# Transposing the gated units of both token halves in one run of eight, in the first four chunks of every feed-forward layer

## The chip, the core and the metric

The kernel runs on one core of a Trainium2 chip. TensorE (PE in the profile) multiplies and transposes and writes PSUM, eight banks of 128 x 512 fp32. PEld is TensorE's loading of the stationary operand, which overlaps PE. VectorE (DVE) and ScalarE (ACT) read PSUM and work on SBUF. SyncE (SP) issues nearly all transfers, and GpSimd (POOL) a few. The metric is the device time of one execution in microseconds; lower is better.

## The reference, cut to what matters

Two stacks run on 256 tokens of width 1024 in fp32. Six token mixers (convolutions, pooling, attention, mLSTM) stand between eight feed-forward layers, and the change touches these eight alone:

```
f = (silu(h @ w_gate) * (h @ w_up)) @ w_down      # h: 256 x 1024, hidden width 2816
```

Before and after each feed-forward layer there is an RMS norm and a residual sum.

## The kernel before, in words

Precision. TensorE works with fp32r operands. Every fp32 operand is split into a high part (a cast on ACT) and a low part (a subtraction on DVE), and every product is three matmuls: high by high, low of the activations by high of the weights, high by low (`mm3`, L282 to L284, in this order). Weights are split on the fly: a raw tile of 1 MB arrives by DMA (L150), ACT casts it in two halves (L229), DVE subtracts in two halves (L190).

Feed-forward. The hidden width is cut into five chunks of 512 and one of 256. The tokens are two halves of 128, h = 0 and h = 1. For a chunk c, gate and up products are made for both halves, ACT and DVE turn them into gated units `s` (128 tokens x 512), and `hidden` transposes each half's `s` in four 128 x 128 blocks into one PSUM bank (L511), splits the bank into high and low (ACT L291, then DVE L292) and gives the bank back. The result is the stationary operand of `down(c, h)`, which is worked off in the middle of the next chunk. Chunk 0 is made by `gate_up`, chunks 1 and 3 by `both`, chunks 2 and 4 (`SUMS`) by `seven`: seven products instead of eight, of operands that DVE adds beforehand. These sums of weight tiles are `pre_add` (DVE L181, in place on a raw tile, when both raw tiles have landed).

What sets the order. There is no planner. Each triple of matmuls is a tick; a tick may issue one step of the weights' splitting, and then runs every task whose delay is over. `hidden` starts such a task, 11 ticks after its half's gated units in chunks 0, 1 and 3, 12 in chunks 2 and 4, 3 in the last chunk. `down` joins the task before it uses its result. Every engine takes its instructions in the order in which they were issued, so a subtraction L292 stands on DVE behind whatever weight step was issued before it, also when that step still waits for a transfer.

Buffers. `ps` are the eight banks, `r2` six tiles for split units (two per half), `f2` ten tiles for units, `r8` nineteen tiles for raw and split weights. All are handed out first come, first served, so a bank that comes back is soon written again: in `seven`, the third product's bank Y (`Y = self.ps.get()`) is one that the chunk before had transposed into.

Of the kernel before, what the change touches and what calls it, by code (L numbers as in the profile page):

```python
# [28 lines left out]
SUMS = (2, 4)  # L29
# [21 lines left out]
class Core:  # L51
# [443 lines left out]
    def ffn(self, plan, half, nxt):  # L495
# [6 lines left out]
        hT, tt = {}, {}  # L502

        def hidden(s, c, h, n, delay):

            def T():
                while not self.ps.free or len(self.r2.free) < 2:
                    yield 1
                b = self.ps.get()
                for j in range(n // 128):  # L510
                    nc.tensor.transpose(out=b[:, j * 128:(j + 1) * 128], in_=s[:, j * 128:(j + 1) * 128], identity=self.ident)  # L511
                self.f2.put(s)
                hT[c, h] = (self.r2.get(), self.r2.get())
                self.split(hT[c, h][0][:, 0:n], hT[c, h][1][:, 0:n], b[:, 0:n])
                self.ps.put(b)
                yield
            tt[c, h] = self.spawn(T(), delay)

        def gate_up(c, h):
            if c < 5:  # L520
                banks = [self.ps.get(), self.ps.get()]
                for i, p in enumerate(G[c]):
                    w = self.need(p)
                    for k in range(4):
                        kk = 4 * (i % 2) + k
                        self.mm3(banks[i // 2], self.lhs(xT, kk, h), (w[0][:, k], w[1][:, k]), kk == 0, kk == 7)
                    if h:
                        self.done(p)
                gb, ub, n = banks[0], banks[1], 512
            else:  # L530
                b = self.ps.get()
                banks = [b]
                for i, p in enumerate(G[c]):
                    w = self.need(p)
                    for k in range(4):
                        kk = 4 * i + k
                        self.mm3(b, self.lhs(xT, kk, h), (w[0][:, k], w[1][:, k]), kk == 0, kk == 7)
                    if h:
                        self.done(p)
                gb, ub, n = b[:, 0:256], b[:, 256:512], 256  # L540
            s = self.f2.get()
            nc.scalar.activation(out=s[:, 0:n], in_=gb, func=ACTF.Silu, scale=rr[h])
            nc.vector.scalar_tensor_tensor(out=s[:, 0:n], in0=ub, scalar=rr[h], in1=s[:, 0:n], op0=ALU.mult, op1=ALU.mult)
            self.ps.put(*banks)
            hidden(s, c, h, n, 11 if c < 5 else 3)

        def both(c):

            s = {}

            def half_chunk(q, use):
                b = [self.ps.get(), self.ps.get()]
                for i in range(2):
                    p = G[c][2 * q + i]
                    w = self.need(p)
                    for h in range(2):
                        for k in range(4):
                            kk = 4 * i + k
                            self.mm3(b[h], self.lhs(xT, kk, h), (w[0][:, k], w[1][:, k]), kk == 0, kk == 7)
                        if i:  # L560
                            self.spawn(use(h, b[h]), 1)
                    self.done(p)

            def gate(h, b):
                s[h] = self.f2.get()
                nc.scalar.activation(out=s[h], in_=b, func=ACTF.Silu, scale=rr[h])
                self.ps.put(b)
                yield

            def up(h, b):  # L570
                nc.vector.scalar_tensor_tensor(out=s[h], in0=b, scalar=rr[h], in1=s[h], op0=ALU.mult, op1=ALU.mult)  # L571
                self.vector(512)
                self.ps.put(b)
                hidden(s[h], c, h, 512, 11)
                yield

            for q, use in enumerate((gate, up)):
                half_chunk(q, use)
                for h in range(2):
                    down(c - 1, h, (q,))  # L580

        def seven(c):


            U = G[c]
            X, Z = self.ps.get(), self.ps.get()
            left = {"a11": lambda k: self.lhs(xT, k, 0), "a12": lambda k: self.lhs(xT, 4 + k, 0), "a22": lambda k: self.lhs(xT, 4 + k, 1)}
            for j, n in enumerate(("s1", "s2", "s4", "s3")):
                left[n] = lambda k, j=j: tuple(t[:, j * 512 + k * 128:j * 512 + k * 128 + 128] for t in self.xs)

            def product(b, n, a, first=False):
                w = self.need(U[n])
                for k in range(4):
                    self.mm3(b, left[a](k), (w[0][:, k], w[1][:, k]), first and k == 0, k == 3, more=not first)
                self.done(U[n])

            f = {}

            def copy(n, b):
                f[n] = self.f2.get()  # L600
                nc.scalar.copy(out=f[n], in_=b)  # L601
                yield

            def gate0():
                nc.vector.tensor_tensor(out=f["1"], in0=Z, in1=f["1"], op=ALU.add)
                self.vector(512)
                self.ps.put(Z)
                nc.scalar.activation(out=f["1"], in_=f["1"], func=ACTF.Silu, scale=rr[0])
                yield

            def up0():
                nc.vector.tensor_tensor(out=f["2"], in0=Y, in1=f["2"], op=ALU.add)
                self.vector(512)
                self.ps.put(Y)
                nc.vector.scalar_tensor_tensor(out=f["2"], in0=f["2"], scalar=self.nr[0], in1=f["1"], op0=ALU.mult, op1=ALU.mult)
                self.vector(512)
                self.f2.put(f["1"])
                hidden(f["2"], c, 0, 512, 12)
                yield

            def up1():
                nc.vector.tensor_tensor(out=f["5"], in0=X, in1=f["5"], op=ALU.add)
                self.vector(512)
                yield

            def gate1():
                g = self.f2.get()
                nc.scalar.activation(out=g, in_=X, func=ACTF.Silu, scale=rr[1])
                self.ps.put(X)
                nc.vector.scalar_tensor_tensor(out=f["5"], in0=f["5"], scalar=self.nr[1], in1=g, op0=ALU.mult, op1=ALU.mult)  # L630
                self.vector(512)
                self.f2.put(g)
                hidden(f["5"], c, 1, 512, 12)
                yield

            product(X, "b11", "a11", True)
            e1 = self.spawn(copy("1", X), 2)
            product(Z, "b21", "a12", True)
            self.join(e1)
            e2 = self.spawn(gate0(), 2)  # L640
            Y = self.ps.get()
            product(Y, "t1", "s1", True)
            e3 = self.spawn(copy("5", Y), 2)
            product(X, "t2", "s2")
            e4 = self.spawn(copy("2", X), 2)
            down(c - 1, 0, (0,))
            self.join(e2, e3)
            product(Y, "b22", "s4")
            self.join(e4)
            e5 = self.spawn(up0(), 2)  # L650
            product(X, "t3", "s3")
            e6 = self.spawn(up1(), 0)
            down(c - 1, 1, (0,))
            down(c - 1, 0, (1,))
            down(c - 1, 1, (1,))
            self.join(e5, e6)
            product(X, "t4", "a22")
            if c == SUMS[-1]:
                self.join(self.spawn(gate1()))
            else:  # L660
                self.spawn(gate1(), 1)
# [22 lines left out]
        def end(h):  # L684
            self.chain(h, acc[h], half, nxt, [lambda: self.ps.put(*acc[h])])

        gate_up(0, 0)
        self.join(self.xt[1])
        rr[1] = self.rr[1]
        gate_up(0, 1)  # L690
        self.ahead = 5
        for c in range(1, 5):
# [11 lines left out]
        down(4, 0)  # L704
        self.limit, self.ahead = 6, 4
        gate_up(5, 0)
        down(4, 1, (0,))
        gate_up(5, 1)
# [1035 lines left out]
```

## Time and profile before

| | us |
|---|---|
| three runs | 2118.84, 2120.30, 2120.38 (median 2120.3) |
| the profiled execution | 2121.1 |
| its span | 2119.1 |
| PE busy | 2094.2 (99%) |
| PEld busy | 1691.5 (80%) |
| DVE busy | 1558.0 (74%) |
| ACT busy | 1213.0 (57%) |
| DMA queue of the weights | 372.04 MB, 50.2% of the 16 engines |

How to read it: the profiled execution took 2121.1 us, of which 2119.1 are the span from the first to the last instruction. A share is a mean over the whole run; whether a particular instruction is late is read in the timeline. A matmul's recorded length (some 400 ns) is longer than the distance to the next one's start (some 233 ns), because matmuls overlap. So the idle time in front of a late matmul is shorter than what its lateness costs.

### The profile page before, as it was taken

The page shows a single profiled execution, that of the slowest core. Times are in us where ns is not written, and L with a number is a line of the kernel's source. Part 1 is how long each engine was busy: PE and PEld are TensorE (multiplying, and loading weights), DVE is VectorE, ACT ScalarE, POOL GpSimd, SP SyncE. Part 2 cuts the span into 40 slices and gives each one's busy share as a digit, 9 for nine tenths or more (in the row PEclk, how much of TensorE's full clock was granted, in tenths as well). Part 3 has the DMA queues.
Part 4 walks back from the last instruction along what each step waited for, and adds up shares of the span by engine and source line. Part 5 has one row for each costly group of instructions (what it writes and reads, how often), then busy time and mean ns, then how long its engine had stood idle before and what let it go on. Part 6 is the DMA issues. An engine that isn't in the chain of part 4 may idle for free. (4 is left out here: it accounts for less than half of the span.)

```text
span 2119.1 us, 25044 instructions
## 1 busy us (share of the span) xinstructions
PE 2094.2 (99%) x9659; PEld 1691.5 (80%) x9659; DVE 1558.0 (74%) x2017; ACT 1213.0 (57%) x1742; POOL 73.7 (3%) x129
## 2 busy tenths in 40 slices
PE   9999999999999999999999999999999999999998
PEld 6877777887888888888888887878888878787887
DVE  5678678876577776678777774787778776479775
ACT  5565456655665555556555456775556545667553
POOL 0000000000000000000000002010000001000000
PEclk9999999999999999999999999999999999999999
DMA  7555554646444564545555464344564545344542
GB/s 279 201 186 196 182 198 151 226 164 222 143 142 173 212 226 162 197 169 199 198 189 177 151 236 163 120 144 174 209 225 162 209 176 184 130 167 161 179 164 95
DMA packets 175623, 383.75 MB, mean 181 GB/s; under 512 B 10428, under 2 KB 29116, under 8 KB 175504
## 3 DMA queue, kind: packets, MB, share of 16 engines
q1 hardware_dynamic: 172592, 372.04, 50.2%
q0 software_dynamic: 2624, 9.58, 1.3%
q8 instruction: 76, 1.25, 0.2%
q10 hardware_dynamic: 288, 0.52, 0.1%
q14 instruction: 43, 0.35, 0.1%
HBM read 380.28 MB, written 1.84 MB: 180 GB/s over the span
## 5 line engine op out<-in xcount | busy, mean ns | idle before, releaser
L282 PE MATMUL ps<-r,r 128*128 128x512 f32 (+1 forms) x2748 | 1100.6, 400 | 2.2 <-ACT f L601 2.2
L283 PE MATMUL ps<-r,r 128*128 128x512 f32 (+1 forms) x2748 | 1082.9, 394 | 3.9 <-DVE r L292 2.6
L284 PE MATMUL ps<-r,r 128*128 128x512 f32 (+1 forms) x2748 | 1080.6, 393 | 2.4 <-DVE r L190 2.4
L190 DVE TENSOR_TENSOR r<-r,r 128x1024 fp32r<-128x1024 f32 x798 | 935.5, 1216 | 167.2 <-ACT r L229 164.4
L229 ACT CAST r<-r 128x1024 fp32r<-128x1024 f32 x798 | 791.8, 1043 | 377.7 <-DVE r L181 163.2
L284 PEld LDWEIGHTS ps<-r,r 128*128 128x128 f32 x2748 | 515.6, 188 | 124.6 <-DVE r L190 7.0
L283 PEld LDWEIGHTS ps<-r,r 128*128 128x128 f32 x2748 | 516.0, 188 | 122.2 <-DVE r L292 11.9
L282 PEld LDWEIGHTS ps<-r,r 128*128 128x128 f32 x2748 | 516.2, 188 | 115.2 <-ACT f L601 2.6
L181 DVE TENSOR_TENSOR r<-r,r 128x1024 f32<-128x1024 f32 x128 | 150.9, 1220 | 57.6 <-DMA r<-in_ffn_w_in_dram 30.3
L291 ACT CAST r<-ps 128x512 fp32r<-128x512 f32 (+1 forms) x108 | 60.0, 555 | 153.2 <-PE ps L511 144.5
L292 DVE TENSOR_TENSOR r<-ps,r 128x512 fp32r<-128x512 f32 (+1 forms) x108 | 69.5, 646 | 89.8 <-ACT r L291 89.8
L571 DVE SCALAR_TENSOR_TENSOR f<-ps,rr,f 128x512 f32<-128x512 f32 x32 | 23.9, 747 | 75.5 <-PE ps L284 75.5
L291 ACT CAST r<-f 128x512 fp32r<-128x512 f32 x84 | 51.4, 619 | 44.2 <-DVE f L376 26.4
L312 POOL TENSOR_TENSOR st<-st,c_mhalf 128x1 f32<-128x1 f32 x28 | 15.9, 569 | 1551.8 <-DVE st L311 1551.4
L316 ACT ACTIVATE c_junk<-x 128x512 bf16<-128x512 f32 x56 | 35.3, 631 | 54.4 <-DVE x L349 53.5
L292 DVE TENSOR_TENSOR r<-f,r 128x512 fp32r<-128x512 f32 x84 | 55.7, 688 | 3.2 <-ACT r L291 0.8
L511 PEld LDWEIGHTS ps<-c_ident,f 128*128 128x128 f32 x352 | 44.3, 140 | 13.2
L511 PE MATMUL ps<-c_ident,f 128*128 128x128 f32 x352 | 54.0, 272 | 0.0
L376 DVE TENSOR_TENSOR f<-ps,c_pre 128x512 f32<-128x512 f32 x52 | 33.5, 685 | 24.3 <-PE ps L302 24.3
L349 DVE SCALAR_TENSOR_TENSOR x<-f,st,x 128x512 f32<-128x512 f32 x56 | 39.6, 749 | 2.5 <-POOL st L312 0.9
L316 ACT ACTIVATE c_junk<-ps 128x512 bf16<-128x512 f32 x52 | 31.0, 597 | 17.0 <-PE ps L284 16.2
L341 DVE TENSOR_TENSOR f<-ps,gn 128x512 f32<-128x512 f32 x52 | 35.5, 683 | 6.7 <-ACT c_junk L316 6.7
(194 smaller groups left out, 940.3 us busy)
## 6 DMA issues: line engine op xcount, KB each, us to landing
r<-in_ffn_w_in_dram SPq DMA_DIRECT2D x80, 1024.0 KB, 5.3
r<-in_ffn_w_down_dram SPq DMA_DIRECT2D x44, 1024.0 KB, 6.2
r<-in_ffn_w_out_dram SPq DMA_DIRECT2D x44, 1024.0 KB, 7.2
r<-in_ffn_w_gate_dram SPq DMA_DIRECT2D x40, 1024.0 KB, 5.3
r<-in_ffn_w_up_dram SPq DMA_DIRECT2D x40, 1024.0 KB, 5.8
r<-in_mix_w_in_dram SPq DMA_DIRECT2D x28, 1024.0 KB, 5.1
r<-in_conv_w_in_dram SPq DMA_DIRECT2D x22, 1024.0 KB, 5.3
r<-in_attn_w_qkv_dram SPq DMA_DIRECT2D x12, 1024.0 KB, 5.3
```

Of the source, the lines that this page charges most:

```text
L181: self.nc.vector.tensor_tensor(out=a[:, sl], in0=a[:, sl], in1=b[:, sl], op=ALU.add)
L190: eng.tensor_tensor(out=lo, in0=raw, in1=hi.bitcast(F32), op=ALU.subtract)
L229: self.nc.scalar.copy(out=hi[:, sl], in_=raw)
L282: mm(out=out, lhsT=x[0], rhs=w[0], start=first, stop=False, skip_group_check=more)
L283: mm(out=out, lhsT=x[1], rhs=w[0], start=False, stop=False, skip_group_check=more)
L284: mm(out=out, lhsT=x[0], rhs=w[1], start=False, stop=last, skip_group_check=more)
L291: self.nc.scalar.copy(out=hi, in_=src)
L292: self.nc.vector.tensor_tensor(out=lo, in0=src, in1=hi.bitcast(F32), op=ALU.subtract)
L316: self.nc.scalar.activation(out=self.junk[:, 0:src.shape[-1]], in_=src, func=ACTF.Square, scale=scale, accum_out=acc)
L341: mul = lambda n: nc.vector.tensor_tensor(out=mg[n], in0=src[n], in1=g[:, n * 512:(n + 1) * 512], op=ALU.mult)
L349: nc.vector.scalar_tensor_tensor(out=xs, in0=mg[n], scalar=r, in1=xs, op0=ALU.mult, op1=ALU.add)
L511: nc.tensor.transpose(out=b[:, j * 128:(j + 1) * 128], in_=s[:, j * 128:(j + 1) * 128], identity=self.ident)
```

## The change

`hidden_pair` takes the place of `hidden` in chunks 0 to 3. It keeps the units of h = 0 until those of h = 1 are ready, then starts one task with the delay that each half had. The task waits until two banks and four `r2` tiles are free, transposes both halves one after the other (through `transpose4`, whose line is L302), and then issues both splits. Chunk 4 and the last chunk keep `hidden`. Whichever half's `down` comes first joins the one task.

```
+        pair = {}
+
+        def hidden_pair(s, c, h, delay):
+
+            pair[h] = s
+            if not h:
+                return
+
+            def T():
+                while len(self.ps.free) < 2 or len(self.r2.free) < 4:
+                    yield 1
+                done = []
+                for i in range(2):
+                    done.append((i, self.transpose4(pair[i])))
+                for i, b in done:
+                    self.f2.put(pair.pop(i))
+                    hT[c, i] = (self.r2.get(), self.r2.get())
+                    self.split(hT[c, i][0], hT[c, i][1], b)
+                    self.ps.put(b)
+                yield
+            tt[c, 0] = tt[c, 1] = self.spawn(T(), delay)
...
-            hidden(s, c, h, n, 11 if c < 5 else 3)
+            if c < 5:
+                hidden_pair(s, c, h, 11)
+            else:
+                hidden(s, c, h, n, 3)
...
-                hidden(s[h], c, h, 512, 11)
+                hidden_pair(s[h], c, h, 11)
...
-                hidden(f["2"], c, 0, 512, 12)
+                if c == SUMS[-1]:
+                    hidden(f["2"], c, 0, 512, 12)
+                else:
+                    hidden_pair(f["2"], c, 0, 12)
...
-                hidden(f["5"], c, 1, 512, 12)
+                if c == SUMS[-1]:
+                    hidden(f["5"], c, 1, 512, 12)
+                else:
+                    hidden_pair(f["5"], c, 1, 12)
```

No instruction is added or removed on any engine; rows move. Below, the second feed-forward layer stands for all eight, in which the places are the same.

DVE, end of chunk 2, before. `r2_5_3161` is the low part of the units of h = 1, `r2_1_3059` (the first row) that of h = 0; `r8` are weights.

```order
L292 TENSOR_TENSOR r2_1_3059<-ps_3_3053,r2_0_3058 128x512
L190 TENSOR_TENSOR r8_16_3050<-r8_3_3009,r8_4_3049 128x1024 x2
L190 TENSOR_TENSOR r8_14_3079<-r8_10_3026,r8_8_3078 128x1024
L630 SCALAR_TENSOR_TENSOR f2_9_2932<-f2_9_2932,rr1_2501,f2_0_3095 128x512
L190 TENSOR_TENSOR r8_14_3079<-r8_10_3026,r8_8_3078 128x1024
L190 TENSOR_TENSOR r8_18_3107<-r8_0_3073,r8_13_3106 128x1024 x2
L190 TENSOR_TENSOR r8_12_3136<-r8_3_3104,r8_5_3135 128x1024 x2
L181 TENSOR_TENSOR r8_3_3104<-r8_3_3104,r8_0_3133 128x1024 x2
L292 TENSOR_TENSOR r2_5_3161<-ps_3_3155,r2_4_3160 128x512
```

The same place after (the lines after the new function have moved by 25 and more; L658 is L630). `r2_1_3157` is now the low part of h = 0.

```order
L190 TENSOR_TENSOR r8_16_3053<-r8_3_3009,r8_11_3052 128x1024 x2
L190 TENSOR_TENSOR r8_14_3070<-r8_10_3029,r8_8_3069 128x1024 x2
L658 SCALAR_TENSOR_TENSOR f2_9_2930<-f2_9_2930,rr1_2501,f2_0_3092 128x512
L190 TENSOR_TENSOR r8_4_3089<-r8_0_3067,r8_13_3088 128x1024 x2
L190 TENSOR_TENSOR r8_12_3127<-r8_3_3086,r8_5_3126 128x1024 x2
L181 TENSOR_TENSOR r8_3_3086<-r8_3_3086,r8_0_3124 128x1024 x2
L292 TENSOR_TENSOR r2_1_3157<-ps_1_3146,r2_0_3156 128x512
L292 TENSOR_TENSOR r2_5_3161<-ps_7_3151,r2_4_3160 128x512
```

The subtraction of h = 0 has moved behind eight halves of weight subtractions and behind the two pre-adds L181.

PE at the same place, after: the run of eight, the first three of the nine matmuls that follow it, and the first three of `down(2, 0)`, which read `r2_0_3156` and `r2_1_3157`.

```order
L302 MATMUL ps_1_3146<-c_ident_71,f2_8_2952 128x128 x4
L302 MATMUL ps_7_3151<-c_ident_71,f2_9_2930 128x128 x4
L282 MATMUL ps_0_3082<-r8_9_3017,r8_1_2374 128x512
L283 MATMUL ps_0_3082<-r8_9_3017,r8_17_2375 128x512
L284 MATMUL ps_0_3082<-r8_7_3018,r8_1_2374 128x512
...
L282 MATMUL ps_2_2701<-r8_15_3034,r2_0_3156 128x512
L283 MATMUL ps_2_2701<-r8_15_3034,r2_1_3157 128x512
L284 MATMUL ps_2_2701<-r8_18_3035,r2_0_3156 128x512
```

Before, the four transposes of h = 0 stood 57 matmuls further ahead, with 70 matmuls between them and the first reader; the four of h = 1 stood where the second half of the run stands now, with 21 matmuls to theirs.

DVE, chunk 1 to chunk 2 of the first feed-forward layer, before: `r2_5_1332` is h = 0, `r2_1_1365` h = 1.

```order
L292 TENSOR_TENSOR r2_5_1332<-ps_5_1326,r2_4_1331 128x512
L190 TENSOR_TENSOR r8_11_1343<-r8_4_1340,r8_16_1342 128x1024
L181 TENSOR_TENSOR r8_6_1245<-r8_6_1245,r8_2_1247 128x1024 x2
L190 TENSOR_TENSOR r8_11_1343<-r8_4_1340,r8_16_1342 128x1024
L292 TENSOR_TENSOR r2_1_1365<-ps_2_1359,r2_0_1364 128x512
```

And after:

```order
L190 TENSOR_TENSOR r8_11_1334<-r8_4_1331,r8_16_1333 128x1024
L181 TENSOR_TENSOR r8_6_1245<-r8_6_1245,r8_2_1247 128x1024 x2
L190 TENSOR_TENSOR r8_11_1334<-r8_4_1331,r8_16_1333 128x1024
L292 TENSOR_TENSOR r2_5_1361<-ps_5_1350,r2_4_1360 128x512
L292 TENSOR_TENSOR r2_1_1365<-ps_2_1355,r2_0_1364 128x512
```

The subtraction that empties the bank of h = 0 has moved behind four weight steps. That bank is now the one that Y gets, 12 matmuls after the run of eight.

## Rows read from the trace of the kernel before

**Rows 1.** The page: busy time, share of the span, instructions.
```profile
PE 2094.2 (99%) x9659; PEld 1691.5 (80%) x9659; DVE 1558.0 (74%) x2017; ACT 1213.0 (57%) x1742; POOL 73.7 (3%) x129
```

**Rows 2.** Waits of PE: who waited for whom, us in total, times, longest.
```profile
PE ps L302 <- DVE x L349: 3.1, 3, 1.9
PE ps L302 <- DVE r L806: 3.0, 1, 3.0
PE ps L283 <- DVE r L292: 2.6, 4, 1.1
...
PE ps L282 <- ACT f L601: 2.2, 1, 2.2
```

**Rows 3.** Timeline of PE, second layer, end of chunk 2: start, length, instruction.
```profile
419.45 0.39 PE L284 MATMUL ps<-r,r 128*128 128x512 f32 x1
419.68 0.60 PE L511 MATMUL ps<-c_ident,f 128*128 128x128 f32 x4
...
420.59 0.39 PE L284 MATMUL ps<-r,r 128*128 128x512 f32 x1
...
422.44 0.39 PE L283 MATMUL ps<-r,r 128*128 128x512 f32 x1
...
425.00 0.39 PE L282 MATMUL ps<-r,r 128*128 128x512 f32 x1
425.46 0.50 PE L283 MATMUL ps<-r,r 128*128 128x512 f32 x1
425.81 0.39 PE L284 MATMUL ps<-r,r 128*128 128x512 f32 x1
```

**Rows 4.** Timeline of PE, a run of eight transposes elsewhere in the kernel.
```profile
113.37 0.39 PE L284 MATMUL ps<-r,r 128*128 128x512 f32 x1
113.60 1.03 PE L302 MATMUL ps<-c_ident,x 128*128 128x128 f32 x8
...
114.94 0.40 PE L284 MATMUL ps<-r,r 128*128 128x512 f32 x1
```

**Rows 5.** Timeline of DVE, second layer, end of chunk 2; idle before, releaser.
```profile
422.45 2.36 DVE L181 TENSOR_TENSOR r<-r,r 128x1024 f32<-128x1024 f32 x2 [2.73 <-DMA r<-in_ffn_w_up_dram]
424.73 0.68 DVE L292 TENSOR_TENSOR r<-ps,r 128x512 fp32r<-128x512 f32 x1
```

**Rows 6.** Timeline of SP's DMA issues, same place.
```profile
416.58 0.37 SPq L150 DMA_DIRECT2D r<-in_ffn_w_up_dram  x1
```

**Rows 7.** Last layer, same place: PE, then DVE.
```profile
2029.70 0.40 PE L283 MATMUL ps<-r,r 128*128 128x512 f32 x1
...
2031.64 0.68 DVE L292 TENSOR_TENSOR r<-ps,r 128x512 fp32r<-128x512 f32 x1
```

**Rows 8.** First layer, chunk 1 to 2: ACT, DVE, PE (Y's first matmul).
```profile
175.91 2.00 ACT L229 CAST r<-r 128x1024 fp32r<-128x1024 f32 x2 [4.15 <-DMA r<-in_ffn_w_down_dram]
...
181.54 0.68 DVE L292 TENSOR_TENSOR r<-ps,r 128x512 fp32r<-128x512 f32 x1
...
176.97 0.40 PE L282 MATMUL ps<-r,r 128*128 128x512 f32 x1
```

**Rows 9.** Second layer, chunk 1 to 2: PE, ACT, DVE, PE (Y's first matmul).
```profile
378.21 0.40 PE L283 MATMUL ps<-r,r 128*128 128x512 f32 x1
...
379.80 2.00 ACT L229 CAST r<-r 128x1024 fp32r<-128x1024 f32 x2
...
385.43 0.68 DVE L292 TENSOR_TENSOR r<-ps,r 128x512 fp32r<-128x512 f32 x1
...
385.09 0.40 PE L282 MATMUL ps<-r,r 128*128 128x512 f32 x1
```

**Rows 10.** Windows after three PE waits: length, engines' busy us, PEclk (granted), DMA.
```profile
33.60:37.00 3.40, 3.26 (x10) 2.79 (x11) 0.10 (x3) 2.11 (x4) 0.00 (x0) 0.50 1.05 387
...
316.90:320.30 3.40, 3.37 (x14) 2.81 (x13) 3.31 (x8) 2.86 (x7) 0.00 (x0) 0.50 0.02 5
...
187.60:191.00 3.40, 3.35 (x14) 2.74 (x15) 3.40 (x4) 3.40 (x5) 0.00 (x0) 1.00 1.05 391
```

## The prediction

> **What bounds the kernel now.** I read the page's busy shares first, then PE's waits, then the timeline around the transposes on PE, DVE and ACT, last the granted clock. TensorE is busy 99% of the span [rows 1], and all its waits together are some 16 us; the four that matter here are in [rows 2]. So a change can win only what TensorE's own instructions cost less, plus a few us of waits, and it can lose wherever an operand comes later than TensorE wants it. Both questions are about single places, not about shares.
>
> **The transposes themselves.** In [rows 3] the reader is to see a run of four between two L284: from 419.45 to 420.59, 1.14 us with three matmul steps in it. The eight steps from 420.59 to 422.44 take 1.85 us, 0.231 each, so the run costs 1.14 - 0.69 = 0.45 us. The run of eight in [rows 4] costs 114.94 - 113.37 - 0.69 = 0.88 us by the same sum. Twice four is 0.90, once eight 0.88: a run has no fixed price that could be saved. 32 runs are merged (four chunks, eight layers), which gives 32 x 0.02 = 0.6 us at most, within the rounding of the rows, and I take 0. The Trainium skill, page "TensorE: Matmul & The Clock Gate", section "Part 4: PE-mode transpose", gives about 275 ns for one transpose in a kernel, most of it access latency. If every run paid that latency once, merging would save 32 x (0.275 - 0.109) = 5.3 us, an estimate from that page; the trace disagrees, since its run of eight costs what two of four do.
>
> **What comes later: chunk 2.** The subtraction of h = 0 (L292) now stands on DVE where that of h = 1 stood, behind two pre-adds L181 that waited 2.73 us for a transfer [rows 5]. That transfer was issued at 416.58 [rows 6], so it took until 422.4. In the second layer L292 ended at 424.73 + 0.68 = 425.41, and its reader on PE, the L283, started 0.05 later, at 425.46 [rows 3]. For h = 1 this was nearly in time: 21 matmuls lay between its transposes and `down(2, 1)`. For h = 0 there are only nine, then an L282, which needs the high part alone (ACT's cast, long done), and then the L283 that needs the low part. Counted from the run, which ends where it ended, that L283 is the one at 422.44 [rows 3]. Nothing else can go ahead on TensorE, and all of `down` is queued behind it.
>
> How late is L292 after the change? In chunk 1, where h = 0's cast went ahead of the weight cast at 379.80, the weight's buffer was free when the L283 of 378.21 ended, at 378.61 [rows 9]. With that cast out of the way the weight cast can start at 378.65, 1.15 us earlier. DVE has one L292 more to do behind it (0.60 from start to start), so its stream runs some 0.55 us ahead as it enters chunk 2. DVE hardly idles from there to the issue of the transfer, so I let all of the 0.55 reach the L181. Then L283 starts at 425.46 - 0.55 = 424.91, 2.47 us late, and 0.1 is lost at the matmul behind it, which came 0.35 after the late one instead of 0.23 [rows 3]: 2.6 us. In the last layer: 2031.64 + 0.68 + 0.05 - 0.55 - 2029.70 + 0.1 = 2.2 us [rows 7]. The same working gives 2.3 to 3.0 us in the five layers between, and for the first I take the second's 2.6. Sum of eight: 21.2 us. Ends: 25.6 if nothing of the 0.55 arrives, 16.4 if all 1.15 does (8 x 0.6 less).
>
> What goes: the late L283 of h = 1, 2.6 us of idle time in four waits [rows 2]. Each also cost about 0.26 beyond its idle time: at 425.46, with hardly any idle time, 0.46 + 0.35 went by for two steps of 0.23. With three more that show as no wait: 4.4 us. h = 1's subtraction now ends 0.6 behind h = 0's, and its reader comes 12 matmuls, 2.8 us, behind h = 0's, so it is in time.
>
> **What comes later: the bank in chunks 1 and 3.** Y's first matmul now overwrites the bank of h = 0, so it waits for that L292. In the second layer it stands at 385.09. The L292 takes the place of the one at 385.43 less the 1.15 that the casts gain: 384.28, done at 384.96 [rows 9]. It is in time by 0.1 us, and I count 0 for the 15 places that look like this. If the casts gain nothing, each is 385.43 + 0.68 + 0.05 - 385.09 = 1.07 late, 16 us in all.
>
> The first layer's chunk 1 differs: its casts wait for a transfer [rows 8], so nothing is gained. L292 ends at 182.22, Y waits from 176.97 to 182.27: 5.3 us. In return the 2.2 us wait for ACT L601 [rows 2], soon after, goes with its 0.26: net 2.9.
>
> Chunk 0 has 15 matmuls, 3.5 us, to the first reader, and the L292 there stands behind no pre-add; 0.
>
> **The clock.** TensorE's granted clock was at half, 0.50 (1.2 GHz), for 3.4 us after the idle time of 3.0 and of 1.9 us, but stayed at full after that of 2.2 [rows 2, 10]. The new waits idle TensorE for about 1.9 to 2.8 us, one for 5, in the middle of plain matmuls. Two of three waits of this size fell, so I let six of nine fall. Half the clock for 3.4 us loses at most 1.7; the window at half holds 10 matmuls instead of 14 [rows 10], 1.0 us. I take 1.2, since a stretch may begin while TensorE still waits: 7 us. Ends: 0 and 9 x 1.7 = 15.
>
> **Sum.** 0 + 21.2 - 4.4 + 2.9 + 0 + 7 = 26.7 us on the profiled execution's 2121.1: 2147.8. The median of the runs is 0.8 below that execution, so 2147.
>
> **Rivals.**
> - Short waits, no fall of the clock. The transfers of chunk 2 run ahead by more than 0.55, since DVE is rid of h = 0's L292 in chunk 2 as well (0.6) and the cast gains 1.15. With 1.15 + 0.6 the eight waits sum to 21.2 - 8 x 1.2 = 11.6, too short to lower the clock: 11.6 - 4.4 + 2.9 = 10, so 2130. For it: DVE works with few gaps there. Against: that L292 is behind the issue that begins the chain.
> - Everything at its upper end: no gain (25.6), every wait lowers the clock (15): 25.6 - 4.4 + 2.9 + 15 = 39, so 2159. For it: two of three waits that are shown fell. Against: the 2.2 did not, and the casts have a visible gap to move into. If the bank waits come on top, more.
> - Faster: the pre-adds' transfer is issued so early that L181 no longer waits. It decides at about 2.5 us: if L181 starts before 420, h = 0's L292 is in time, and what stays are the 4.4 saved and a saving of the run: 2121.1 - 4.4 - 0.6 less 0.8 for the median = 2115. For it: DVE idles 2.73 before L181. Against: the tile that the transfer fills comes free by a DVE subtraction, whose own tile came by a transfer too, so the chain is as long as before.
> - No change: what is lost at chunk 2 is given back by later waits that vanish. All of PE's waits are 16 us, and most of them stand between layers [rows 2], where the new waits change nothing; 2121.
> - The change doing nothing is excluded: the rows of the order have the runs of eight.
>
> **Chances and range.** Forecast 58% (its own range 2138 to 2154), short waits 16%, upper end 15%, faster 6%, no change 5%. For the range I reach from the short waits to the upper end, 2130 to 2159, which leaves out the last two and what lies beyond the ends. A measurement here can tell some 0.2%, 4.2 us. Faster by more than that 0.06, within 0.06, slower 0.88.
>
> **What would show it.** PE's waits should have L283 <- DVE L292 eight times, about 2.3 us of idle each, in place of four with 2.6 in all; on DVE, both L292 of chunk 2 right behind the pair of L181 that waits for a DMA. In the first layer L282 should wait 5 us for L292 where Y begins, and the wait for L601 be gone. The runs of eight should still cost 0.88 us. The granted clock should show several new stretches at 0.50. I am wrong if L181 starts as soon as TensorE needs it, if the runs of eight are cheaper than 0.8 us, or if Y waits in most layers.

## The result and the profile after

| | median, us | lowest to highest | runs |
|---|---|---|---|
| before | 2119.14 | 2117.49 to 2120.38 | 6 |
| after | 2167.53 | 2164.90 to 2170.65 | 6 |

The ratio is 1.0226, with a 95% interval of 1.0215 to 1.0237: slower by 48 us, where 27 were forecast, and 8.5 us above the range. The profiled execution of the changed kernel took 2165.12 us, its span is 2163.1, 44.0 us longer than before. These 44.0 us are what the rows below have to account for. This execution is the second shortest of the six, 2.4 us under their median.

The page's busy line after (answers to [rows 1]):

```profile
PE 2109.2 (98%) x9659; PEld 1701.8 (79%) x9659; DVE 1559.0 (72%) x2017; ACT 1210.7 (56%) x1742; POOL 73.7 (3%) x129
```

No engine has an instruction more or less. PE is busy 15.0 us longer with the same 9659 instructions, so some of them ran slower, and the remaining 29 us of the span are idle time of PE.

PE's waits after (who waited for whom, us in total, times, longest; answers to [rows 2]):

```profile
PE ps L283 <- DVE r L292: 28.5, 9, 4.8
PE ps L282 <- DVE r L292: 4.7, 1, 4.7
```

These two rows are new in size; the wait of L282 for ACT L601 (2.2 us) is gone, and the rest, which is not shown, stands as before within 0.6 us. Eight of the nine waits in the first row are `down(2, 0)`, one in each layer, 28.3 us together; the ninth (0.2 us) lies elsewhere. The second row is Y's bank in the first layer.

PE in the second layer, end of chunk 2, after (start, length, instruction, idle before and releaser; answers to [rows 3]):

```profile
423.99 0.39 PE L284 MATMUL ps<-r,r 128*128 128x512 f32 x1
424.22 1.03 PE L302 MATMUL ps<-c_ident,f 128*128 128x128 f32 x8
425.01 0.48 PE L282 MATMUL ps<-r,r 128*128 128x512 f32 x1
425.32 0.39 PE L283 MATMUL ps<-r,r 128*128 128x512 f32 x1
...
427.18 0.39 PE L282 MATMUL ps<-r,r 128*128 128x512 f32 x1
430.88 0.80 PE L283 MATMUL ps<-r,r 128*128 128x512 f32 x1 [3.31 <-DVE r L292]
431.48 0.63 PE L284 MATMUL ps<-r,r 128*128 128x512 f32 x1
431.90 0.63 PE L282 MATMUL ps<-r,r 128*128 128x512 f32 x1
```

Three things are to be seen. The run of eight costs 425.32 - 423.99 = 1.33 us with two matmul steps of 0.233 in it, so 0.87. The L283 comes 3.70 us behind the L282 instead of 0.23, so 3.47 us late, where 2.47 were forecast for this layer. And behind it the distance from matmul to matmul is 0.42 instead of 0.23: TensorE's clock has fallen, as the granted clock below shows.

DVE in the same place after (answers to [rows 5]):

```profile
419.77 0.75 DVE L658 SCALAR_TENSOR_TENSOR f<-f,rr,f 128x512 f32<-128x512 f32 x1 [2.05 <-ACT f L656]
420.44 4.62 DVE L190 TENSOR_TENSOR r<-r,r 128x1024 fp32r<-128x1024 f32 x4
427.87 2.36 DVE L181 TENSOR_TENSOR r<-r,r 128x1024 f32<-128x1024 f32 x2 [2.81 <-DMA r<-in_ffn_w_up_dram]
430.14 1.28 DVE L292 TENSOR_TENSOR r<-ps,r 128x512 fp32r<-128x512 f32 x2
```

SP's issue of the transfer that L181 waits for, after (answers to [rows 6]):

```profile
422.82 0.37 SPq L150 DMA_DIRECT2D r<-in_ffn_w_up_dram  x1
```

The chain is the forecast one (transfer, two L181, two L292, then `down(2, 0)`), but it begins later. The clearest mark to measure it from is the matmul that follows the transposes, at 425.01 after and at 420.03 before:

```profile
420.03 0.48 PE L282 MATMUL ps<-r,r 128*128 128x512 f32 x1
```

Before, the transfer was issued 3.45 us ahead of that matmul and L181 began 2.42 behind it [rows 5, 6]. After, it was issued 2.19 ahead, so 1.26 later, and L181 began 2.86 behind. The transfer itself took less time (427.87 - 422.82 = 5.05 against 5.87 by the same sum), which gave 0.82 of the 1.26 back.

What held it back is on ACT. First ACT before at this place, then after:

```profile
410.84 0.69 ACT L628 ACTIVATE f<-ps,rr 128x512 f32<-128x512 f32 x1 [0.73 <-PE ps L284]
413.10 2.00 ACT L229 CAST r<-r 128x1024 fp32r<-128x1024 f32 x2 [1.57 <-DMA r<-in_ffn_w_down_dram]
```

```profile
418.10 1.05 ACT L229 CAST r<-r 128x1024 fp32r<-128x1024 f32 x1 [3.64 <-DMA r<-in_ffn_w_down_dram]
419.05 0.68 ACT L656 ACTIVATE f<-ps,rr 128x512 f32<-128x512 f32 x1
419.63 1.04 ACT L229 CAST r<-r 128x1024 fp32r<-128x1024 f32 x1
```

L656 is L628, the silu of h = 1. Before, it stood ahead of the weight cast that waits for a transfer. After, it stands between the cast's two halves, so it waits with the cast. The cast itself begins where it did, 6.9 us ahead of the mark in both traces. On DVE, L658 needs it (2.05 us of idle time), and the L190 behind L658 are what empties the tile that SP's issue at 422.82 fills. The order that stands ahead of the prediction does not show ACT, but it shows the counterpart of this swap on DVE: L630 stood between the two halves of a subtraction (`r8_14`), and L658 stands behind both. A tick in which h = 0's transposes used to stand now issues a weight step instead, and the weights' splitting is one step further when the silu comes.

Y's bank in the first layer, PE after (answers to [rows 8]):

```profile
181.80 0.79 PE L282 MATMUL ps<-r,r 128*128 128x512 f32 x1 [4.70 <-DVE r L292]
```

4.70 us of idle time, and Y's first matmul starts 4.86 us late where 5.3 were worked out. In the other 15 places of this kind Y does not wait.

Granted clock after, in stretches that follow PE waits (length, engines' busy us, then PEclk; answers to [rows 10]):

```profile
430.50:433.90 3.40, 3.02 (x7) 2.44 (x8) 3.19 (x4) 0.00 (x0) 0.00 (x0) 0.50 0.00 0
433.90:437.30 3.40, 3.40 (x16) 2.74 (x16) 0.00 (x0) 0.00 (x0) 0.00 (x0) 1.00 0.00 0
1017.60:1024.40 6.80, 5.67 (x13) 4.51 (x14) 3.94 (x5) 0.00 (x0) 0.00 (x0) 0.50 0.00 0
```

At 0.50 (1.2 GHz) the matmuls start 0.43 us apart, at full clock 0.233. The first of these stretches, of which 0.4 us are still idle, holds 7 of them, the next one at full clock 16. In the whole trace, seven of the eight waits of chunk 2 and the one for Y's bank are followed by such a stretch, and three of these last 6.8 us. Some begin while TensorE still waits.

The account of the 44.0 us of span: the waits of chunk 2, each by how late its L283 starts plus the 0.1 at the matmul behind it, summed over eight layers, 30.4; less the old waits of h = 1 by the same sum, 4.4; Y's bank, net, 2.5; together 28.5. The remainder, 15.5, is what the clock can have taken. It fits the 15.0 us by which PE is busy longer, and an experiment below prices it apart.

### The profile page after: what moved, and what is told of

Its sections match the earlier page's. It is cut to its first block, busy times and chain, and to the rows that moved or that the text cites. A ratio compares the mean times of both kernels' runs of the same rounds, so it can differ in the third digit from the quotient of the medians.

```text
span 2163.1 us, 25068 instructions
## 1 busy us (share of the span) xinstructions
PE 2109.2 (98%) x9659; PEld 1701.8 (79%) x9659; DVE 1559.0 (72%) x2017; ACT 1210.7 (56%) x1742; POOL 73.7 (3%) x129
## 5 line engine op out<-in xcount | busy, mean ns | idle before, releaser
L283 PE MATMUL ps<-r,r 128*128 128x512 f32 (+1 forms) x2748 | 1089.2, 396 | 29.6 <-DVE r L292 28.5
L282 PE MATMUL ps<-r,r 128*128 128x512 f32 (+1 forms) x2748 | 1103.8, 402 | 5.3 <-DVE r L292 4.7
L190 DVE TENSOR_TENSOR r<-r,r 128x1024 fp32r<-128x1024 f32 x798 | 933.9, 1216 | 227.2 <-ACT r L229 225.1
L283 PEld LDWEIGHTS ps<-r,r 128*128 128x128 f32 x2748 | 519.5, 189 | 150.3 <-DVE r L292 38.2
L282 PEld LDWEIGHTS ps<-r,r 128*128 128x128 f32 x2748 | 519.4, 189 | 123.8 <-DVE r L292 8.2
L181 DVE TENSOR_TENSOR r<-r,r 128x1024 f32<-128x1024 f32 x128 | 150.8, 1220 | 52.5 <-DMA r<-in_ffn_w_up_dram 26.8
L292 DVE TENSOR_TENSOR r<-ps,r 128x512 fp32r<-128x512 f32 (+1 forms) x108 | 66.7, 644 | 57.9 <-ACT r L291 57.8
L302 PEld LDWEIGHTS ps<-c_ident,f 128*128 128x128 f32 x464 | 55.5, 140 | 16.9 <-DVE r L837 3.2
L302 PE MATMUL ps<-c_ident,f 128*128 128x128 f32 x464 | 64.9, 273 | 3.8 <-DVE r L837 2.8
L292 DVE TENSOR_TENSOR r<-f,r 128x512 fp32r<-128x512 f32 x84 | 55.6, 687 | 3.1 <-ACT r L291 0.7
L349 DVE SCALAR_TENSOR_TENSOR x<-f,st,x 128x512 f32<-128x512 f32 x56 | 39.6, 749 | 2.5 <-POOL st L312 0.9
```

What stands on the lines that cost most here:

```text
L181: self.nc.vector.tensor_tensor(out=a[:, sl], in0=a[:, sl], in1=b[:, sl], op=ALU.add)
L190: eng.tensor_tensor(out=lo, in0=raw, in1=hi.bitcast(F32), op=ALU.subtract)
L282: mm(out=out, lhsT=x[0], rhs=w[0], start=first, stop=False, skip_group_check=more)
L283: mm(out=out, lhsT=x[1], rhs=w[0], start=False, stop=False, skip_group_check=more)
L292: self.nc.vector.tensor_tensor(out=lo, in0=src, in1=hi.bitcast(F32), op=ALU.subtract)
L302: self.nc.tensor.transpose(out=b[:, j * 128:(j + 1) * 128], in_=src[:, j * 128:(j + 1) * 128], identity=self.ident)
```

## The experiments

All ratios are to the kernel before, run beside it on the same chip. Where two versions from different rows are compared below, note that the kernel before itself differs by up to 1.6 us between chips.

| kernel | pairs in chunks | median, us | before, us | ratio, 95% |
|---|---|---|---|---|
| e1_not_chunk2 | 0, 1, 3 | 2130.96 | 2119.43 | 1.0052 (1.0036 to 1.0069) |
| e2_only_chunk2 | 2 | 2163.87 | 2119.43 | 1.0211 (1.0195 to 1.0226) |
| e3_charge | all four, silu put back | 2151.40 | 2119.43 | 1.0155 (1.0140 to 1.0171) |
| e4_fill | all four, filler matmuls | 2153.14 | 2119.43 | 1.0158 (1.0143 to 1.0174) |
| e5_before_early | none, chunk 2 after 5 ticks | 2117.17 | 2120.46 | 0.9987 (0.9979 to 0.9996) |
| e6_pair_early | all four, chunk 2 after 5 ticks | 2130.91 | 2120.46 | 1.0051 (1.0039 to 1.0063) |
| e7_only_chunk1 | 1 | 2134.79 | 2120.46 | 1.0070 (1.0056 to 1.0084) |
| e8_chunks0_3 | 0, 3 | 2122.47 | 2120.46 | 1.0009 (1.0001 to 1.0018) |
| e9_only2_delay8 | 2, after 8 ticks | 2117.86 | 2118.90 | 0.9995 (0.9986 to 1.0004) |
| e10_pair_delay8 | all four, chunk 2 after 8 ticks | 2122.38 | 2118.90 | 1.0016 (1.0007 to 1.0024) |

My theory after the result: nearly all of the loss is chunk 2's. It consists of L292 queued behind weight steps that wait for a transfer, of a silu that makes this transfer later, and of the clock that falls in the wait. The rival: merging costs wherever it is done, through eight transposes in a row, two banks held at once and two splits in a row.

### Which chunk: e1 and e2

e1 takes chunk 2 out of the change, e2 leaves only chunk 2 in it.

```
-                if c == SUMS[-1]:                       # e1, same for h = 1
-                    hidden(f["2"], c, 0, 512, 12)
-                else:
-                    hidden_pair(f["2"], c, 0, 12)
+                hidden(f["2"], c, 0, 512, 12)
...
-                hidden_pair(s[h], c, h, 11)             # e2, same in gate_up
+                hidden(s[h], c, h, 512, 11)
```

Expected of e1:

> Runs of eight in chunks 0, 1 and 3; chunk 2 keeps its two runs of four. Theory: nearly the whole loss is the wait of down(2, 0) for the low part of h = 0 in chunk 2, with what the clock does after it. Then 2121 to 2123 us: the kernel before plus 2.5 us for the bank wait in the first layer. Rival: the runs of eight themselves, or the bank waits in chunks 1 and 3, cost it. Then three of four parts of the loss stay, over 2150 us.

Expected of e2:

> The reverse: a run of eight in chunk 2 alone. Theory: 2163 to 2167 us, eight waits of L283 for L292 of 3 to 4 us and most of the half-speed stretches. Rival (runs of eight or banks in the other chunks): below 2130 us.

Measured: e2 2163.87, as expected; chunk 2 alone costs 44.4 us, and its waits of L283 for L292 are 30.7 us. e1 2130.96: most of the loss is gone, but 11.5 us stay, where I expected two or three. Its waits:

```profile
PE ps L283 <- DVE r L292: 7.0, 9, 1.8
PE ps L282 <- DVE r L292: 4.9, 2, 4.6
```

The second row is Y's bank, as expected (4.6 of the 4.9). The first is the surprise: but for 0.2 us these are the waits of h = 1 in chunk 2, which e1 did not touch, and they have grown from 2.6 to 6.8 us. So a pair in chunk 0, 1 or 3 makes something in chunk 2 later. The losses do not add up (44.4 + 11.5 against 48.4). That fits the waits that grow in e1: the pair in chunk 2 removes them.

### The silu: e3

After the change, with one task more in chunk 2, at the tick where h = 0's transposes used to stand. It issues no instruction; it only tells the kernel's own bookkeeping that VectorE is taken for 512 columns, so that no weight step is issued at that tick. The silu then stands ahead of the cast again. By the traces, two instructions per layer change their place: the silu goes ahead of half a cast on ACT, and its product (L658) ahead of half a subtraction on DVE. The order of all others, PE's included, is that of the changed kernel.

```
             pair[h] = s
             if not h:
+                if c == SUMS[0]:
+                    def charge():
+                        self.vector(512)
+                        yield
+                    self.spawn(charge(), delay)
                 return
```

> The changed kernel, but at the tick at which h = 0 of chunk 2 was transposed before, 512 columns are entered in the account of DVE's time that holds the weight splitting back; nothing else. The silu of h = 1 then stands on ACT ahead of both halves of the next weight cast again, as in the kernel before, not between them. Theory: the waits are about 1 us longer than forecast because the silu stood behind a cast that waits for a transfer, and the subtraction that frees the tile for the next transfer stood behind the silu's product. Then the transfer is issued about 1 us earlier again relative to the run, each of the eight waits is 0.5 to 1.3 us shorter, and the time is 2152 to 2160. Rival: the transfers alone were slower in the changed kernel; then the waits and 2165 to 2169 us stay.

Measured 2151.40, 16 us less than after and 0.6 below the expected range: the theory's side. ACT, then SP, then PE in the second layer, and PE's wait as a whole:

```profile
417.31 0.69 ACT L661 ACTIVATE f<-ps,rr 128x512 f32<-128x512 f32 x1 [0.94 <-PE ps L284]
420.03 2.00 ACT L229 CAST r<-r 128x1024 fp32r<-128x1024 f32 x2 [2.04 <-DMA r<-in_ffn_w_down_dram]
```

```profile
423.50 0.37 SPq L150 DMA_DIRECT2D r<-in_ffn_w_up_dram  x1
```

```profile
426.93 0.48 PE L282 MATMUL ps<-r,r 128*128 128x512 f32 x1
...
431.72 0.50 PE L283 MATMUL ps<-r,r 128*128 128x512 f32 x1 [2.23 <-DVE r L292]
```

```profile
PE ps L283 <- DVE r L292: 21.2, 9, 3.5
```

The silu runs before the cast, and the transfer is issued 3.43 us ahead of the matmul behind the transposes (426.93) instead of 2.19. That is where it was before (3.45), so in this layer the silu accounts for the whole delay of the issue. L283's wait is 2.23 us instead of 3.31. Over the kernel, L283 waits 21.2 us for L292 instead of 28.5. That saves 7.3 us of waiting. Of the other 9 the clock is the part that can be seen: it falls in four new places instead of eight. So the two terms that I had too small hang together: here, with waits some 0.9 us longer each, more of them were followed by a slow stretch.

### The clock by itself: e4

After the change, with twelve matmuls more ahead of each `down(2, 0)`. They write a bank that nobody reads, and only keep TensorE at work while L292 is late. ACT and DVE keep the order of the changed kernel.

```
+                if c == 3 and q == 0:
+                    ds = [self.ps.get() for _ in range(3)]
+                    for _ in range(12):
+                        nc.tensor.matmul(out=ds[2], lhsT=xT[0][:, 0:128], rhs=xT[0][:, 0:512], start=True, stop=True)
+                    self.ps.put(*ds)
```

> The changed kernel with twelve matmuls of 128x512 added in front of down(2, 0) in every layer, written to a bank that nobody reads: 2.8 us of TensorE's work in the place where it waits. Theory: about a third of the loss, some 15 us, is time at half clock after the idle wait. With the wait filled the clock stays at full, the rest of the wait is under 1.5 us, and the time falls to 2150 to 2157 although 96 matmuls are added. Rival: the clock costs little; then 2166 to 2170.

Measured 2153.14. The second layer on PE, and the granted clock behind the wait:

```profile
429.15 2.89 PE L607 MATMUL ps<-r 128*128 128x512 f32 x12
...
433.47 0.50 PE L283 MATMUL ps<-r,r 128*128 128x512 f32 x1 [1.21 <-DVE r L292]
```

```profile
433.40:436.80 3.40, 3.33 (x14) 2.75 (x15) 2.88 (x4) 0.00 (x0) 0.00 (x0) 1.00 0.02 5
```

`down` is held up no less: the L283 comes 433.47 - 429.15 = 4.32 us after the point where `down` would begin, against 430.88 - 427.18 = 3.70 in the changed kernel. Yet 96 matmuls of extra work make the kernel 14.4 us shorter (2167.53 - 2153.14), since no stretch at half clock follows the waits of chunk 2 any more. That is the price of the clock, measured apart, and it agrees with the remainder of 15.5. It is good to some 4 us either way, by the two intervals; the two profiled executions alone differ by 10.2. The rest of the waits is not under 1.5 us everywhere, as I expected: the longest is 2.2.

### Whether the pair costs anything where nothing is queued ahead of it: e5, e6, e9 and e10

If L292 is late because of what stands ahead of it on DVE, it is enough to ask for the transposes a few ticks sooner. e5 does this in the kernel before, e6 in the changed one.

```
-                hidden(f["5"], c, 1, 512, 12)            # e5, of before
+                hidden(f["5"], c, 1, 512, 12 if c == SUMS[-1] else 5)
...
-                    hidden_pair(f["5"], c, 1, 12)        # e6, of after
+                    hidden_pair(f["5"], c, 1, 5)
```

> The kernel before with one number changed: in chunk 2 the transposes of h = 1 come 5 ticks behind its gated units instead of 12, so its L292 stands on VectorE ahead of the L190 and the two L181 that wait for the transfer. Theory (L292 is late because it queues behind weight steps that wait for a transfer): the waits L283 <- L292 of 2.6 us and their hidden part go, 2114 to 2117 beside some 2119 for before, and the transfer is issued at most 0.7 us later. Rival (the pre-adds are the late step and push what follows, so the time comes back there): 2119 to 2123, with new waits of L282 or L283 for L190 or L181.

> The changed kernel with the same edit: in chunk 2 the run of eight comes 5 ticks behind the units of h = 1 instead of 12, both L292 ahead of the L190 and the pair of L181. Theory (all of the chunk 2 loss, waits and clock, is the place of the L292 on VectorE): no wait of chunk 2 is left and none of its stretches at half clock; what stays is the bank wait of the first layer with its stretch and the side effect of chunk 1: 2120 to 2128. Rival (merging itself costs, by one run of eight and two splits in a row, wherever it stands): above 2140.

e5: 2117.17, 3.3 us under the kernel before on the same chip (0.8 to 4.5 by the interval): 0.2 above the theory's range and below the rival's, and the one version that is faster than both kernels beyond its interval. DVE in the second layer, then PE's waits:

```profile
415.63 0.69 DVE L292 TENSOR_TENSOR r<-ps,r 128x512 fp32r<-128x512 f32 x1
...
421.30 2.36 DVE L181 TENSOR_TENSOR r<-r,r 128x1024 f32<-128x1024 f32 x2 [2.09 <-DMA r<-in_ffn_w_up_dram]
```

```profile
PE ps L283 <- DVE r L292: 0.2, 1, 0.2
```

L292 runs 5.7 us before L181 instead of behind it, and the four waits, 2.6 us together, are down to one of 0.2.

e6: 2130.91. The waits of L283 for L292 are gone, which is 37 of the 48 us, but the time is 3 us above what I expected. Its longest waits but Y's:

```profile
PE ps L302 <- DVE f L658: 6.4, 7, 2.1
```

I had overlooked that five ticks can be too soon: the run asks for the units of h = 1 before they are there, and they are late for the same reason as above, the silu behind half a cast that waits for a transfer (for 5.05 us in the last layer, where the silu L656 then begins at 2030.08 and the second half of the run, at 2031.61, has waited 2.10 us). So the same edit with 8 ticks, with pairs in chunk 2 alone (e9) and in all four (e10):

```
-                    hidden_pair(f["5"], c, 1, 12)        # e9 on e2, e10 on after
+                    hidden_pair(f["5"], c, 1, 8)
```

> The pair in chunk 2 alone, and its run of eight 8 ticks behind the units of h = 1 instead of 12, so that both L292 stand on VectorE ahead of the L190 and the two L181, and no transpose is asked for before the units are ready. Theory (a merged run costs nothing where its subtractions queue behind nothing): 2115 to 2120, like the kernel before or like its early variant. Rival (merging has a price in chunk 2 by itself, the second split standing behind the first): above 2124.

> The changed kernel, pairs in all four chunks, with 8 ticks instead of 12 in chunk 2. With 5 ticks it took 2130.9, of which 6.4 us were waits of the transposes for the gated units (L302 <- L658) and some 2 more what these hide; with 8 ticks they go. Theory: 2121 to 2126; what is left over before is the bank wait of the first layer with its stretch at half clock. Rival (the rest is a price of chunk 1 that shows as no wait): still 2128 to 2132.

e9: 2117.86, not to be told from the kernel before (2118.90). The same pair, four ticks later, costs 44.4 us (e2). e10: 2122.38, 45 us under the changed kernel with one number changed in it. DVE in the second layer of e10:

```profile
419.08 0.75 DVE L658 SCALAR_TENSOR_TENSOR f<-f,rr,f 128x512 f32<-128x512 f32 x1 [2.17 <-ACT f L656]
...
422.02 1.28 DVE L292 TENSOR_TENSOR r<-ps,r 128x512 fp32r<-128x512 f32 x2
...
427.10 2.36 DVE L181 TENSOR_TENSOR r<-r,r 128x1024 f32<-128x1024 f32 x2 [1.52 <-DMA r<-in_ffn_w_up_dram]
```

L658 still waits 2.17 us for the silu, but nobody waits for it any more: both L292 are done 3.8 us before L181 can start. PE's waits and the clock at Y's bank in e10:

```profile
PE ps L282 <- DVE r L292: 5.0, 1, 5.0
```

```profile
181.20:188.00 6.80, 5.83 (x14) 4.58 (x15) 5.09 (x7) 3.02 (x4) 0.00 (x0) 0.50 0.76 288
```

What e10 has over e9 (2122.38 - 2117.86 = 4.5 us) fits this one place of the first layer: 5.0 us of idle time instead of the 2.2 for ACT, and 6.8 us at half clock, of which 1 is still idle. The rival, a price of merging wherever it is done, falls: by its interval e9 is between 3.0 us faster and 0.8 slower than the kernel before.

### Where e1's 11.5 us come from: e7 and e8

```
-                hidden_pair(s[h], c, h, 11)              # e7; e8 the other way round
+                (hidden_pair(s[h], c, h, 11) if c == 1 else hidden(s[h], c, h, 512, 11))
```

> The pair in chunk 1 alone, chunks 0, 2 and 3 as before. Theory (what chunks 0, 1 and 3 lose together, 11.8 us, comes from chunk 1: Y's bank in the first layer, and a silu that now stands between two halves of a cast and makes the h = 1 of chunk 2 later): 2128 to 2132. Rival (it is shared with chunk 3, whose neighbours look alike): 2123 to 2126.

> The pair in chunks 0 and 3, chunks 1 and 2 as before. Theory: 2118 to 2121, no new wait, the waits L283 <- L292 at the 2.6 us of before. Rival (chunk 3 has a price of its own, as its L292 of h = 0 is as far behind as in chunk 1): 2124 to 2128.

e7: 2134.79, 14.3 us over before (11.9 to 17.8), 2.8 us above the expected range: chunk 1 alone loses about as much as the three pairs of e1. e8: 2.0 us over (0.2 to 3.8), 1.5 above the expected range. It has no wait above 0.4 us that the kernel before does not have, and L283 waits 1.1 us for L292 where I expected 2.6. But its granted clock is 0.50 from 188.80 to 192.20, behind a wait of 2.11 us for ACT, where the kernel before stayed at full behind 2.17 [rows 10]. At 0.43 us a matmul instead of 0.233 such a stretch costs some 1.6 us, an estimate. So whether chunks 0 and 3 cost 2 us or nothing stays open. PE's waits for L292 at L283 in e7, and one of them with the granted clock behind it:

```profile
PE ps L283 <- DVE r L292: 7.7, 8, 2.0
```

```profile
434.77 0.50 PE L283 MATMUL ps<-r,r 128*128 128x512 f32 x1 [2.02 <-DVE r L292]
```

```profile
436.20:439.60 3.40, 3.40 (x10) 2.63 (x9) 0.98 (x2) 1.27 (x2) 0.00 (x0) 0.50 0.02 5
```

Chunk 1's pair has a place of its own, Y's bank in the first layer, and one at a distance: the waits of h = 1 in chunk 2 grow by 5.1 us, and two of them, of 2.02 us each, are followed by a fall of the clock. In the changed kernel the reason can be read at chunk 1, ACT and then DVE of the second layer:

```profile
390.06 1.05 ACT L229 CAST r<-r 128x1024 fp32r<-128x1024 f32 x1 [1.47 <-issue]
391.17 0.73 ACT L633 ACTIVATE f<-f,rr 128x512 f32<-128x512 f32 x1
391.80 1.03 ACT L229 CAST r<-r 128x1024 fp32r<-128x1024 f32 x1
```

```profile
395.21 1.23 DVE L190 TENSOR_TENSOR r<-r,r 128x1024 fp32r<-128x1024 f32 x1 [1.11 <-ACT r L229]
```

Here, too, a silu (L633, of h = 0) has come between two halves of a weight cast, and DVE waits for the second half. That this is what makes chunk 2 later in e7 is read from this trace, not tried. That chunk 1's distant price exists only through chunk 2's queue is shown by e10, where the pair in chunk 1 stays and the price goes.

## Why the prediction was too low, step by step

- **A run has no fixed price: right.** 0.87 us for eight, as in [rows 4], and e9 is not faster than before by anything that can be told. The 275 ns that the Trainium skill, page "TensorE: Matmul & The Clock Gate", section "Part 4: PE-mode transpose", gives for one transpose are the length of one instruction, and the trace agrees: 272 ns is the median length of the transposes L511 in the kernel before. As a price they do not hold: the transposes of a run overlap, and eight cost 0.87 us, 109 ns each.
- **L292 of h = 0 in chunk 2 becomes late in every layer: right in place and mechanism, wrong in size.** 30.4 us against 21.2. The step that failed is "DVE hardly idles from there to the issue of the transfer, so I let all of the 0.55 reach the L181". DVE does idle there, in two places, and both are waits for ACT. The first stood in the trace of before, and I had passed over it:

```profile
390.26 1.23 DVE L190 TENSOR_TENSOR r<-r,r 128x1024 fp32r<-128x1024 f32 x1 [1.11 <-ACT r L229]
```

After, the same L190 starts at 395.21, again after 1.11 us of idle time (row above, behind the silu L633): 4.95 us later, while TensorE came 4.98 later. So nothing of the 0.55 is left there in the second layer, although both L292 of chunk 1 ran as early as forecast. A run shows what the gain was worth: e2 has no pair in chunk 1 and so no gain, and its L283 waits 30.7 us against 28.5. That is 2.2 us in eight layers instead of 4.4, most of it in one layer (5.35 against 3.58). The second place is new: DVE waits 2.05 us for the silu L656, and the transfer is issued 1.26 later than before, measured from the transposes. e3 prices it: with the silu put back L283 waits 7.3 us less. There L181 begins 1.77 behind the transposes, against 2.42 before and 2.86 after, and L283 is 2.39 late in the second layer where 2.47 were forecast. That is luck: the issue is where it was before, not 0.55 earlier, and the transfer took 0.67 less. I had bounded the term by "nothing of the gain arrives" (25.6); that the chain could become slower than before was not among the ends.
- **The old waits of h = 1 go: right** (4.4 us; e5 measures their removal alone with 3.3, interval 0.8 to 4.5).
- **Y's bank: right.** 2.5 us net against 2.9 in the first layer, and none in the other 15 places.
- **The clock: wrong in size.** I let six of nine waits lower it, at 1.2 us each, 7 us. Eight of nine did, three of them for 6.8 us, and matmuls started 0.43 us apart instead of 0.233: 14.4 us by e4, 15.5 by the remainder. My window for the price, the first of [rows 10], had ten instructions at half clock, but four of them were transposes, which are shorter than full matmuls; so half clock looked cheaper than it is for plain matmuls.
- **The rivals.** "Everything at its upper end" (2159) was nearest: its 25.6 for the waits does not reach, and its clock term of 15 holds in size, but partly by luck, since it was nine falls of 1.7 and not eight of which three are double. The short waits, the faster kernel and the unchanged one are excluded by the rows of L283.

Neither error alone leaves the range: with 30.4 for the waits and my 7 for the clock the sum is 2156, with 21.2 and 14.4 it is 2154. With all the measured terms, e4's for the clock, it is 30.4 - 4.4 + 2.5 + 14.4 = 42.9 of the 44.0 us between the profiled executions. The median is another 2.4 above the profiled execution, where I had put it 0.8 below; that is no error of a term.

## What to carry to other kernels

When a task moves to another tick of an in-order program, read the order of every engine for what slips past it, not only where the moved instructions go: here one silu that changed places with half a weight cast was worth 16 us, and a delay of 8 ticks instead of 12 was worth 45. Before a gain upstream is credited to a late instruction, follow the chain between them; an instruction on the way that waits for another engine can take the gain away (here the L190 that waits 1.11 us for ACT's cast). And price a wait of TensorE with the clock that may fall behind it: here 14.4 us on waits of 30.4, about half as much again.

## What the runs showed of the hardware

The length of a wait alone does not tell whether TensorE's clock falls. Two waits of e3 on PE, and the granted clock behind each:

```profile
1015.78 0.50 PE L283 MATMUL ps<-r,r 128*128 128x512 f32 x1 [3.07 <-DVE r L292]
...
1724.87 0.79 PE L283 MATMUL ps<-r,r 128*128 128x512 f32 x1 [2.35 <-DVE r L292]
```

```profile
1015.80:1019.20 3.40, 3.40 (x15) 2.76 (x16) 2.79 (x3) 0.00 (x0) 0.00 (x0) 1.00 0.00 0
...
1724.50:1727.90 3.40, 3.03 (x7) 2.45 (x8) 3.18 (x4) 0.38 (x1) 0.00 (x0) 0.50 0.00 0
```

After 3.07 us of idle time it stayed at full (1.00), after 2.35 it fell to half (0.50), and in e7 after 2.02. In the changed kernel all waits of 3.3 us and more were followed by a fall, and the one of 2.24 in the first layer was not; in e2 one of 3.5, in the last layer, was not either. Even the same wait in the same place differs from run to run. The wait of L302 for L349 ahead of the second layer took 1.89 us before and was followed by 0.50 (the second of [rows 10]); after the change it took 1.90, and the clock stayed at full:

```profile
321.80:325.20 3.40, 2.53 (x16) 1.84 (x15) 3.31 (x8) 2.86 (x7) 0.00 (x0) 1.00 0.02 5
```

What decides between 1.9 and 3.5 us these rows do not tell, so a forecast does well to keep both ends there.
